# One adaLN sum moved behind a key's low part, and one weight conversion moved ahead of two copies

## The chip, the cores and the metric

The kernel runs on one NeuronCore of a Trainium2 chip. The metric is the device time of one execution in microseconds; before the change it is 1125.85 us, the median of three runs (1125.52 to 1125.99). A separate execution was taken by the hardware profiler, and all rows below come from it.

The engines of the core appear under these names: PE is TensorE (matrix products; PEld is its loading of the stationary operand), DVE is VectorE, ACT is ScalarE, POOL is GpSimd, SP is SyncE, which here only issues DMAs. Each engine works through its own instructions in order, and engines wait for each other by semaphores.

## What is computed

The reference is a two-layer trunk on one sequence of 512 tokens of 1024 channels. Cut to what matters here:

```python
def ada_modulation(c, w, b):
    m = jax.nn.silu(c) @ w + b
    shift, scale, gate = jnp.split(m, 3, axis=-1)
    ...

for i in range(DEPTH):
    shift, scale, gate = ada_modulation(c, mix_ada_w[i], mix_ada_b[i])
    h = rms_norm(x, mix_pre_g[i]) * (1.0 + scale) + shift
    y = stick_breaking_mixer(...) if i % 2 == 0 else token_mixing_mixer(...)
    x = x + gate * rms_norm(y, mix_post_g[i])
    shift, scale, gate = ada_modulation(c, ffn_ada_w[i], ffn_ada_b[i])
    h = rms_norm(x, ffn_pre_g[i]) * (1.0 + scale) + shift
    y = swiglu(h, ffn_w_gate[i], ffn_w_up[i], ffn_w_down[i])
    x = x + gate * rms_norm(y, ffn_post_g[i])
```

The mixer of layer 0 is an attention with 16 heads of 64 channels: q, k and v are products of h with `w_qkv`, the scores are turned into stick-breaking weights by a sigmoid and a running product, and the weighted sum of v goes through `w_o`. Every sublayer needs its own shift, scale and gate, each a product of the conditioning vector (1024) with a 1024 x 1024 matrix.

## The kernel before

All is float32, done on TensorE as sums of products of a high part and a low part: `split` (L109) makes the high part `h` with a copy on ScalarE and the low part `l` as source minus high part on VectorE, and `mm3` (L101) issues three products, h·h, h·l and l·h. So every weight block of 512 KB passes through ScalarE (`wh<-raw`) and VectorE (`wl<-raw`) before TensorE can use it.

**The start.** x comes in as four token tiles of 128 tokens. Each is normed, turned by TensorE into accumulator banks (`tp`, function `turn0`), and copied out by ScalarE (`turned0`) into `xhT`; one call copies the half of a tile in two instructions. Behind the copies of the first halves, ScalarE scales the turned x by the adaLN scale and shift (`high0`: `hTh<-xhT,ab`, then `xhT<-xhT,ab`); VectorE makes the low part of that (`low0`: `hTl<-xhT,hTh`). The scale and shift themselves (`ab`) are sums on VectorE (`ada_row`: `ada<-ada,scr`) over blocks that arrive by DMA (`in_ada0w`). v's first weights (`raw<-in_wv`) are split in two halves; the high part of the first half is `wh<-raw 128x512`, by an explicit instruction at L703. In this part of the program, the order on each engine is that of the code.

**The attention.** Eight pairs of heads go through a loop (`for i in range(NPAIR)`, L973). While pair i is finished, the scores of pair i + 1 are begun. For each of three groups of blocks, TensorE turns the weights of pair i (`flip`: `tw<-pack,ga`, copied out by ScalarE as `ar<-tw`), fills in other products, takes a group of scores for pair i + 1 (`z<-k,q`), which go through ScalarE's sigmoid (`ga<-z`) and VectorE's running product (the scan `ga<-ga,tri`), and fills in again. Behind the three groups stand the weighted sum of v (`values`: `av<-ar,V`) and its split (`finish`: `o<-av`).

The fillers are a generator (`filler`): first the products of q and k of the later pairs in steps of an eighth (`pqk`, read out by `evac_q` and `evac_k`), then the first part of the output product (`y<-wh,o` for two token tiles and four of the eight blocks of `w_o`). The banks for `pqk` and for the first two `y` groups come from the same two accumulator banks (tag `"p"`). `evac_k` writes k's high part on ScalarE and its low part on VectorE, both out of the bank.

The table `FILLS` (L821) says how many filler steps stand in each of the seven places of a pair (places 0 to 5 in the three groups, place 6 behind the split of o). The table `SUMS` (L824) has the same seven places and says how many steps of `bg` are taken there. `bg` computes shift, scale and gate of the first mixer's output and the next sublayer's input: three parts (G0, A0, B0) of eight blocks each, so 24 steps, each one `scalar_tensor_tensor` on VectorE that adds a block `rawada` times a column of `sc` to a running sum (`B<-rawada,sc,B`); then further steps that sum over the partitions with a product (`spare<-acch,ones`). The blocks come through two buffers (tag `raw2`), loaded by POOL's queue; the same two buffers later take the loads `rawy<-in_wy` of the feed-forward stage, issued by SP.

Four of the 24 sums are made before the loop; the loop's pairs 0 to 3 take three each, pairs 4 and 5 four each. So the last sum is the fourth of pair 5. The last filler step of q and k (the last eighth of k of pair 7) is in place 5 of pair 5.

## Time and profile before

| what | us |
|---|---|
| median of three timed runs | 1125.85 |
| the profiled execution, whole | 1127.71 |
| its span on the core | 1125.9 |
| TensorE busy | 1105.2 |
| VectorE busy | 903.2 |
| ScalarE busy | 603.0 |
| POOL busy | 39.8 |

A row of a timeline is: start and length in us, engine, line, operation, output <- inputs, shapes, count, and in brackets the idle time before it and what ended that. The names are those of the program's buffers. A line is often that of a helper (L64 for all of VectorE's and ScalarE's instructions, L90 for products, L107 for DMAs), so instructions are told apart by their buffers. "SPq" is the queue in which SP issues DMAs. A busy TensorE can still be slow: the granted clock of each stretch stands in the windows view.

### The profile page before, as it was taken

Reading aid. Unit: us, or ns where it says so; the run is one execution under the profiler, and the core shown is the slowest. Engines: PE = TensorE matmul, PEld = TensorE weight load, DVE = VectorE, ACT = ScalarE, POOL = GpSimd, SP = SyncE. Lnnn points to the kernel's source line nnn. Section 1 sums busy time; section 2 is a strip of 40 time slices with the busy share of each in tenths; the row PEclk is TensorE's granted clock in tenths of the full one; section 3 lists DMA queues with packets and bytes.
Section 4 is the critical chain, followed back from the end, with each engine's and each line's share of the span. In section 5 each row is a group of like instructions: output and inputs, shape, how many; then the busy total and the mean of one; then the engine's idle time right before and its main releaser. Section 6 shows DMA issues by size and latency. Waiting matters only on the chain.

```text
span 1125.9 us, 18286 instructions
## 1 busy us (share of the span) xinstructions
PE 1105.2 (98%) x7318; PEld 993.6 (88%) x7318; DVE 903.2 (80%) x1161; ACT 603.0 (54%) x977; POOL 39.8 (4%) x71
## 2 busy tenths in 40 slices
PE   6999999999999999999999999999999999999997
PEld 5788878779999999988878988988999999989896
DVE  7777889659988988787687774759988898889986
ACT  7646767647555555562244634437555555556552
POOL 0220111000000000010000000000000000000000
PEclk9999999999999999999999999999999999999999
DMA  9676445353244444368875482333244444223233
GB/s 361 234 216 172 145 144 168 124 187 132 76 149 150 134 132 132 110 215 270 270 255 186 159 298 83 116 113 141 84 151 127 137 132 151 75 76 112 95 94 149
DMA packets 51298, 176.09 MB, mean 156 GB/s; under 512 B 5643, under 2 KB 6155, under 8 KB 50318
## 3 DMA queue, kind: packets, MB, share of 16 engines
q1 hardware_dynamic: 45166, 153.95, 41.4%
q0 software_dynamic: 6048, 20.98, 5.9%
q8 instruction: 57, 0.93, 0.3%
q14 instruction: 27, 0.22, 0.1%
HBM read 164.43 MB, written 8.39 MB: 153 GB/s over the span
## 4 chain that ended last, share of the span: by engine, by line
PE 83%; DMA 8%; DVE 6%; issue 2%; ACT 1%; SPq 0%; POOL 0%; DVEq 0%; POOLq 0%; ACTq 0%
PE r L90 32%; PE y L90 12%; PE X L90 7%; PE v L90 7%; PE gu L90 6%; DMA rawada<-in_ada 5%; PE pqk L90 5%; PE u L90 4%; PE M L90 3%; DMA raw<-in_wdown 1%; PE z L90 1%; PE tw L98 1%; DMA ada<-in_ada0w 1%; PE av L90 1%; PE tp L98 1%
## 5 line engine op out<-in xcount | busy, mean ns | idle before, releaser
L64 ACT ACTIVATE wh<-raw 128x1024 fp32r<-128x1024 f32 (+1 forms) x112 | 116.8, 1051 | 140.9 <-PE y L90 42.0
L64 DVE TENSOR_TENSOR wl<-raw,wh 128x1024 fp32r<-128x1024 f32 (+1 forms) x112 | 134.9, 1211 | 61.9 <-ACT wh L64 61.8
L90 PE MATMUL r<-Sh,wh 128*128 128x256 f32 x608 | 170.2, 280 | 0.2 <-ACT e L64 0.2
L90 PE MATMUL r<-Sh,wl 128*128 128x256 f32 x608 | 170.4, 280 | 0.0
L90 PE MATMUL r<-Sl,wh 128*128 128x256 f32 x608 | 170.1, 280 | 0.0
L90 PE MATMUL y<-wh,as 128*128 128x512 f32 x480 | 153.3, 396 | 0.1
L64 DVE TENSOR_TENSOR wl<-f,wh 128x1024 fp32r<-128x1024 f32 x76 | 92.7, 1220 | 35.8 <-ACT wh L64 35.8
L64 ACT ACTIVATE wh<-f 128x1024 fp32r<-128x1024 f32 x76 | 80.6, 1061 | 67.9 <-PE r L90 65.1
L90 PEld LDWEIGHTS r<-Sh,wh 128*128 128x128 f32 x608 | 114.7, 189 | 0.4 <-ACT e L64 0.4
L90 PEld LDWEIGHTS r<-Sl,wh 128*128 128x128 f32 x608 | 114.6, 188 | 0.0
L90 PEld LDWEIGHTS r<-Sh,wl 128*128 128x128 f32 x608 | 114.6, 188 | 0.0
L90 PEld LDWEIGHTS y<-wh,as 128*128 128x128 f32 x480 | 90.1, 188 | 21.5 <-DVE G L64 0.6
L90 PE MATMUL y<-wl,as 128*128 128x512 f32 x240 | 94.9, 395 | 0.0
L90 PE MATMUL r<-hTh,wh 128*128 128x256 f32 x304 | 88.8, 292 | 0.2 <-DVE gu L64 0.2
L90 PE MATMUL r<-hTl,wh 128*128 128x256 f32 x304 | 84.8, 279 | 0.0
L90 PE MATMUL r<-hTh,wl 128*128 128x256 f32 x304 | 80.1, 280 | 0.0
L90 PE MATMUL X<-wh,as 128*128 128x512 f32 (+1 forms) x272 | 76.3, 356 | 0.0
L64 ACT ACTIVATE e<-r 128x256 f32<-128x256 f32 x114 | 43.4, 382 | 51.6 <-PE r L90 51.2
L90 PEld LDWEIGHTS r<-hTh,wh 128*128 128x128 f32 x304 | 57.2, 188 | 5.4 <-DVE gu L64 1.3
L90 PE MATMUL r<-hTh,b 128*128 128x256 f32 x304 | 60.7, 282 | 0.0
L64 ACT ACTIVATE wh<-rawx 128x1024 fp32r<-128x1024 f32 x38 | 40.4, 1063 | 35.9 <-PE r L90 30.8
L90 PEld LDWEIGHTS r<-hTl,wh 128*128 128x128 f32 x304 | 57.3, 188 | 0.1
(240 smaller groups left out, 2844.7 us busy)
## 6 DMA issues: line engine op xcount, KB each, us to landing
rawada<-in_ada SPq DMA_DIRECT2D x56, 512.0 KB, 5.1
raw<-in_wdown SPq DMA_DIRECT2D x44, 512.0 KB, 4.1
rawy<-in_wy SPq DMA_DIRECT2D x38, 512.0 KB, 3.6
rawx<-in_wx SPq DMA_DIRECT2D x38, 512.0 KB, 4.5
rawada<-in_ada POOLq DMA_DIRECT2D x24, 512.0 KB, 4.5
raw<-in_wqk SPq DMA_DIRECT2D x16, 512.0 KB, 4.6
ada<-in_ada0w SPq DMA_DIRECT2D x7, 1026.0 KB, 10.8
raw<-in_wgu SPq DMA_DIRECT2D x12, 512.0 KB, 3.6
```

The source lines that it names most:

```text
L64: b = f(*a, **k)
L90: b = nc.tensor.matmul(o, l, r, start=start, stop=stop, skip_group_check=True)
L98: last_tp[0] = nc.tensor.transpose(o, i, ident)
```

## The change

It has two parts. They move instructions and neither add nor remove any.

```diff
@@ -694,13 +694,14 @@
     turn0(3, 0)
     turn0(3, 1)
     ada_row(0, 1)
-    for tt in range(NT):
-        turned0(tt, 0, act)
     w, raw = wtile(2, 512), raws[0]
     wv0.append(w)
     got.append(w)
     taken[0] += 1
-    act.activation(w[0][:, 0, :], raw[:, 0, :], AF.Copy)
+    for tt in range(NT):
+        if tt == NT - 1:
+            act.activation(w[0][:, 0, :], raw[:, 0, :], AF.Copy)
+        turned0(tt, 0, act)
     high0(0)
@@ -821,7 +822,7 @@
-        SUMS = ((1, 0, 1, 0, 1, 0, 0),) * 4 + ((1, 1, 1, 0, 1, 0, 0),) * 2 + ((1, 1, 1, 1, 1, 1, 0), (1, 0, 1, 0, 1, 1, 0))
+        SUMS = ((1, 0, 1, 0, 1, 0, 0),) * 4 + ((1, 1, 1, 0, 1, 0, 0), (1, 1, 1, 0, 0, 0, 1)) + ((1, 1, 1, 1, 1, 1, 0), (1, 0, 1, 0, 1, 1, 0))
```

The first part concerns ScalarE at the start. The difference of its order (- before, + after; `xhT<-tp` are the copies of the turned x, two for each tile, the last two those of tile 3; `wh<-raw` is the high part of v's first weights; buffer numbers are serial and carry no meaning of their own):

```order
 L64 ACTIVATE xhT_117<-tp_49_195 128x2x128
 L64 ACTIVATE xhT_118<-tp_49_195 128x2x128
+L64 ACTIVATE wh_221<-raw_97 128x512
 L64 ACTIVATE xhT_117<-tp_52_209 128x2x128
 L64 ACTIVATE xhT_118<-tp_52_209 128x2x128
-L64 ACTIVATE wh_229<-raw_97 128x512
 L64 ACTIVATE hTh_121<-xhT_117,ab_205 128x512
 L64 ACTIVATE xhT_117<-xhT_117,ab_205 128x512
```

The weights' high part has moved ahead of the two copies of tile 3; what follows keeps its order. VectorE's and TensorE's order at this place is the same in both.

The second part concerns VectorE at the end of pair 5: `B<-rawada,sc,B` are the adaLN sums, `ga<-ga,tri` the scans of pair 6's scores, `k<-pqk,k` the low part of the last k, `o<-av,o` that of pair 5's output:

```order
 L64 SCALAR_TENSOR_TENSOR B_1496<-rawada_1692,sc,B_1496 128x1024
 L64 SCALAR_TENSOR_TENSOR ga_1725<-ga_1725,tri 128x256 x2
+L64 SCALAR_TENSOR_TENSOR ga_1758<-ga_1758,tri 128x512 x2
+L64 TENSOR_TENSOR k_1769<-pqk_1705,k_1769 64x512 x2
+L64 TENSOR_TENSOR o_1786<-av_717,o_1786 128x512
 L64 SCALAR_TENSOR_TENSOR B_1496<-rawada_1718,sc,B_1496 128x1024
-L64 SCALAR_TENSOR_TENSOR ga_1759<-ga_1759,tri 128x512 x2
-L64 TENSOR_TENSOR k_1770<-pqk_1705,k_1770 64x512 x2
-L64 TENSOR_TENSOR o_1787<-av_717,o_1787 128x512
 L64 TENSOR_TENSOR wl_1803<-raw_1706,wh_1802 128x1024
 L64 TENSOR_TENSOR accl_1823<-G_568,acch_1822 128x512
```

The last sum has moved behind two scans, the low part of k and the low part of o. The difference of SP's queue at the same time (`rawy` a block for the feed-forward stage, into the buffers that the `rawada` blocks leave; `g` the gains of two norms; `raw<-in_wo` output weights):

```order
 L107 DMA raw_1800<-in_wo 128x1024
 L107 DMA rawy_2511<-in_wy 128x1024
-L107 DMA rawy_2515<-in_wy 128x1024
 L107 DMA g_1820<-in_post_g 128x1024
 L107 DMA g_1892<-in_pre_g 128x1024
+L107 DMA rawy_2515<-in_wy 128x1024
 L107 DMA raw_2087<-in_wo 128x1024
 L107 DMA raw_2093<-in_wo 128x1024
```

The second `rawy` load now stands behind the two `g` loads. POOL's queue and TensorE's order are the same as before, apart from names.

## The prediction

> **What bounds the kernel now.** I read the busy times first, then what TensorE waits for, then the chain of waits around the longest of those waits, and last the granted clock there.

> ```profile
> PE 1105.2 (98%) x7318; PEld 993.6 (88%) x7318; DVE 903.2 (80%) x1161; ACT 603.0 (54%) x977; POOL 39.8 (4%) x71
> ```

> TensorE is busy for 1105.2 of 1125.9 us. The change moves no matmul, so it can win only where TensorE stands still or runs slowly. Inside the body of the kernel, the list of TensorE's waits has one long entry at the place of the second edit:

> ```profile
> PE y L90 <- DVE k L64: 2.6, 1, 2.6
> ```

> The chain of waits says where it comes from. Columns are start, length, what.

> ```profile
> 193.14 5.16 DMA rawada<-in_ada
> ...
> 203.35 0.14 issue
> 203.48 3.66 PE y L90 x9
> ...
> 231.48 20.98 PE y L90 x90
> ```

> A block of adaLN weights (`rawada`) is issued at 193.14 and lands at 193.14 + 5.16 = 198.30. Everything on the chain from there to 203.48 is VectorE, and from 203.48 it is TensorE again. The last row gives the pace of these products when nothing holds them: 20.98 / 90 = 0.233 us each. Now VectorE's timeline at this place:

> ```profile
> 195.35 1.26 DVE L64 TENSOR_TENSOR_SCAN ga<-ga,tri 128x256 f32<-128x256 f32 x2
> 198.40 1.28 DVE L64 SCALAR_TENSOR_TENSOR B<-rawada,sc,B 128x1024 f32<-128x1024 f32 x1 [1.78 <-DMA rawada<-in_ada]
> 199.60 2.33 DVE L64 TENSOR_TENSOR_SCAN ga<-ga,tri 128x512 f32<-128x512 f32 x2
> 201.94 1.39 DVE L64 TENSOR_TENSOR k<-pqk,k 64x512 fp32r<-64x512 f32 x2
> 203.37 0.69 DVE L64 TENSOR_TENSOR o<-av,o 128x512 fp32r<-128x512 f32 x1
> 203.97 1.22 DVE L64 TENSOR_TENSOR wl<-raw,wh 128x1024 fp32r<-128x1024 f32 x1
> ...
> 208.38 2.34 DVE L64 TENSOR_TENSOR_SCAN ga<-ga,tri 128x512 f32<-128x512 f32 x2 [1.45 <-ACT ga L64]
> ```

> The last adaLN sum (198.40) stands ahead of the scans and of the low part of the last k (201.94). VectorE idles 1.78 us for its weights and spends 1.28 us on it. Only when the second half of k has been read out of the accumulator bank can TensorE start the second group of `y`, which takes that same bank.

> **The change, part by part: the adaLN sum.** The sum goes behind the scans, k and the split of o. Then the scans no longer wait for the DMA. They need ScalarE's sigmoids, and k needs ScalarE's high part:

> ```profile
> 195.20 1.09 ACT L64 ACTIVATE ga<-z 128x512 f32<-128x512 f32 x2 [0.52 <-PE z L90]
> 197.07 1.21 ACT L64 ACTIVATE k<-pqk 64x512 fp32r<-64x512 f32 x2 [0.78 <-PE pqk L90]
> 199.40 0.60 ACT L64 ACTIVATE o<-av 128x512 fp32r<-128x512 f32 x1 [1.12 <-PE av L90]
> 200.82 1.06 ACT L64 ACTIVATE wh<-raw 128x1024 fp32r<-128x1024 f32 x1
> ```

> The sigmoids are done at 196.29 and VectorE at 195.35 + 1.26 = 196.61, where a successor starts some 0.08 before the listed end (199.60 against 198.40 + 1.28), so the scans start at 196.53. k follows 201.94 - 199.60 = 2.34 later, at 198.87, after its high part (197.07 + 1.21 = 198.28), and takes 1.39: 200.26. With the 0.14 of the chain, the bank is free for TensorE at **200.40**. TensorE's own rows:

> ```profile
> 200.46 0.39 PE L90 MATMUL y<-wh,o 128*128 128x512 f32 x1
> ...
> 203.48 0.77 PE L90 MATMUL y<-wh,o 128*128 128x512 f32 x1 [2.63 <-DVE k L64]
> ...
> 206.98 0.22 PE L90 MATMUL z<-k,q 128*128 128x128 f32 x1
> ...
> 210.40 0.40 PE L90 MATMUL y<-wl,o 128*128 128x512 f32 x1
> ```

> The last product ahead of the wait starts at 200.46, the next could start at 200.46 + 0.233 = 200.69, and the bank is free 0.29 before that. **First term: 203.48 - 200.69 = 2.79 us.** The wait vanishes as a whole, with 0.29 to spare.

> Second term: after the wait TensorE is slow. Nine products go from 203.48 to 206.98, 3.50 us, where 9 x 0.233 = 2.10 would do. The windows show why (columns: window, length, busy times, then granted clock, DMA share, GB/s):

> ```profile
> 200.90:203.40 2.50, 0.00 (x0) 0.00 (x0) 2.44 (x4) 2.44 (x4) 0.00 (x0) 0.92 0.82 292
> 203.40:204.00 0.60, 0.52 (x1) 0.50 (x2) 0.60 (x2) 0.00 (x0) 0.00 (x0) 0.50 0.96 246
> ...
> 206.00:206.50 0.50, 0.50 (x2) 0.38 (x2) 0.50 (x1) 0.00 (x0) 0.00 (x0) 0.60 0.79 156
> 206.50:207.00 0.50, 0.50 (x4) 0.39 (x3) 0.43 (x1) 0.00 (x0) 0.00 (x0) 1.00 0.86 188
> ```

> The clock is halved: 0.92 over 2.50 us means the last 0.4 us of the wait, and 0.60 over 0.50 us means up to about 206.4. Half of the 2.9 us between 203.48 and 206.4 is about 1.45, which agrees. **Second term: 3.50 - 2.10 = 1.40 us**, gone if the wait that sets the clock back is gone. Sum: 2.79 + 1.40 = **4.19 us**.

> What is late next? Behind the moved sum on VectorE's queue stand the low part of the fourth output weight (203.97), the low part of G, another weight and the next scans (208.38). o is split from 200.26 to 200.95 (its high part is there at 200.00), the sum runs from 200.87 to 202.15 with its weights long landed, and the low part, which waits for ScalarE's high part (200.82 + 1.06 = 201.88), goes from 202.07 to 203.29. TensorE asks for it at 210.40, or at 206.21 once it is 4.19 earlier: 2.9 us of cover. Then 0.61 and 1.22 us for the two next (0.69 and 1.22 listed) put the scans at 204.97. 208.38 - 4.19 = 204.19 would be their moved time; they come 0.78 late, and their reader on TensorE is the transposing of the next pair, more than 8 us away, so I take nothing for it. On SyncE's queue the second `rawy` load waits for the sum, so it moves from about 199.7 to 202.2, and the two `g` loads pass it; the weight load behind it waits for the low part (205.2 before, 203.3 now). The queue's row, and the first reader of `rawy`:

> ```profile
> 195.46 4.58 SPq L107 DMA_DIRECT2D rawy<-in_wy  x2
> ```

> ```profile
> L64 ACT ACTIVATE b<-rawy x2: 619/620/621, 274.5 to 275.1; 128x512 fp32r<-128x512 f32 x2
> ```

> All these cost nothing while they keep their covers. From 207 on the chain of waits is TensorE up to 252, so 4.19 us travels on.

> **The high part of v's first weights.** It goes ahead of the copies of the last token tile. In order: SyncE's issue, the DMA's time to landing, ScalarE and VectorE.

> ```profile
> 4.24 0.44 SPq L107 DMA_DIRECT2D raw<-in_wv  x1
> ```

> ```profile
> raw<-in_wv SPq DMA_DIRECT2D x1, 512.0 KB, 9.8
> ```

> ```profile
> 14.08 0.66 ACT L64 ACTIVATE xhT<-tp 128x256 f32<-128x256 f32 x2 [0.79 <-PE tp L98]
> 14.62 0.63 ACT L64 ACTIVATE wh<-raw 128x512 fp32r<-128x512 f32 x1
> 15.14 0.81 ACT L64 ACTIVATE hTh<-xhT,ab 128x512 fp32r<-128x512 f32 x1
> 15.99 0.82 ACT L64 ACTIVATE xhT<-xhT,ab 128x512 f32<-128x512 f32 x1
> 16.77 1.23 DVE L64 SCALAR_TENSOR_TENSOR ada<-ada,scr 128x1026 f32<-128x1026 f32 x1 [0.79 <-DMA ada<-in_ada0w]
> 17.92 0.69 DVE L64 TENSOR_TENSOR hTl<-xhT,hTh 128x512 fp32r<-128x512 f32 x1
> ```

> ScalarE idles 0.79 us ahead of 14.08, and the edit means to fill that. But the weights land at 4.24 + 9.8 = 14.04, so ScalarE would wait there instead: high part near 14.08, copies at 14.60, scaled x at 14.60 + 0.66 = about 15.28 instead of 15.14. If they were there at 13.3, scaled x would come near 14.78, 0.36 earlier. Neither matters for the end as I read it: VectorE's queue waits for another load until 16.77 and reaches the low part of x at 17.92, for which ScalarE's 15.99 + 0.82 = 16.81 is 1.1 us early. TensorE's next products need that low part. **Term: 0.** Bounds: VectorE's idle of 0.79 is all that an earlier landing could win (-0.79), and the two copies, now behind the weights, are all that a later one could expose (+0.66). I keep both for the range.

> The profiled execution took 1127.71 us with its span of 1125.9, so it would go to 1127.71 - 4.19 = 1123.52. The three timed runs have a median of 1125.85, 1.86 below it; I take the same difference off that: **1121.66 us**, which is 0.37% less.

> **The rivals.** First, the gap closes, but the timed runs never paid for the clock. A wait of the same length elsewhere left it at full speed (last figure but two of a window):

> ```profile
> 569.92 0.50 PE L90 MATMUL adaps<-acch,ones 128*128 128x512 f32 x1 [2.66 <-ACT acch L64]
> ```

> ```profile
> 569.00:570.00 1.00, 0.08 (x1) 0.08 (x1) 0.62 (x1) 1.00 (x3) 0.00 (x0) 1.00 0.88 356
> ```

> So 2.6 us may or may not halve the clock, and the 1.86 us that the profiled execution is slower could hold these 1.40. Then only 2.79 is won: 1123.06. [...]

> Second, the gain is swallowed later. TensorE's 2.66 us wait at 569.92 ends a stretch in which the chain goes from DMA to DMA. Had that stretch a clock of its own, TensorE would wait there 4.19 longer, and the time stays at 1125.85. But its head hangs on TensorE, so it should start earlier by as much:

> ```profile
> 470.63 12.99 PE r L90 x107
> 483.64 0.13 ACT gu L64
> ```

> Third, slower: the sum keeps waiting for its DMA and now holds up another queue of work.

> ```profile
> DMA to landing us min/median/max: 3.7/4.5/9.9
> ```

> VectorE waits if the weights land after 200.87 (7.7 us after issue), and TensorE if the low part of the fourth weight ends after 206.2, which is a landing after about 203.6, 10.5 us after issue. Each further us costs one; the whole 4.19 is gone at 207.8, 14.7 after issue, and a landing at 211 gives 1125.85 + 3.2 = 1129. For it: the `g` loads may now leave from 195.8 on, while `rawada` is in flight. Against it: 1 MB more at the 292 GB/s of the first window above is 3.6 us, a landing at 201.9 at worst, and the longest of 24 took 9.9.

> **How the numbers follow.** Forecast as summed, 1121.66: 0.50. Clock not paid for, 1123.06: 0.30. Swallowed later, or a new short wait that leaves under 2.25 us of gain: 0.16. Slower: 0.04. A measurement of this kernel can tell about 0.2%, 2.25 us; both of the first cases exceed it. So faster 0.80, same 0.16, slower 0.04. The range runs from 1121.66 - 0.79 = 1120.9 to 1123.06 + 0.66 = 1123.7, opened to 1120.7 and 1123.8 because the three runs themselves lie between 1125.52 and 1125.99.

> **What would show it.** Right: TensorE's list of waits has no `y` behind `k`; k's low part starts near 198.9 with no idle ahead of the scans; the moved sum starts near 200.9; the granted clock stays at 1.00 through 200 to 207, and z starts near 202.8 instead of 206.98. For the first edit: ScalarE's high part starts at about 14.1 behind a DMA wait, with hTl still at 17.9. Wrong: a new wait of TensorE between 203 and 232, a `y` that waits for `wl`, or a wait at 570 that has grown to some 6.9 us.

## The result, and the profile after

The changed kernel takes 1123.2 us, the median of 20 runs (1120.92 to 1124.78); the kernel before takes 1125.4 us in 20 runs (1122.23 to 1127.48). The ratio is 0.9977, with a 95% interval of 0.9970 to 0.9985: 2.6 us won (1.7 to 3.4), where 4.19 were forecast as likeliest and 2.79 as the next case. The two medians by themselves lie 2.2 us apart; the ratio is taken from all the runs. The profiled executions lie further apart, 1122.0 against 1125.9 us of span.

TensorE's list of waits of the changed kernel, in total, times and longest, whole:

```profile
PE sc L90 <- ACT sc L64: 2.9, 1, 2.9
PE v L90 <- ACT hTh L64: 2.5, 3, 1.4
PE tp L98 <- DVE x L64: 2.2, 2, 1.5
PE adaps L90 <- ACT acch L64: 2.0, 1, 2.0
PE v L90 <- DVE hTl L64: 1.3, 2, 0.8
PE r L90 <- ACT e L64: 0.3, 1, 0.3
```

The `y` that waited for `k` is gone from it. VectorE's timeline at the place of the sum:

```profile
195.26 3.50 DVE L64 TENSOR_TENSOR_SCAN ga<-ga,tri 128x256 f32<-128x256 f32 x4
198.77 1.39 DVE L64 TENSOR_TENSOR k<-pqk,k 64x512 fp32r<-64x512 f32 x2
200.19 0.69 DVE L64 TENSOR_TENSOR o<-av,o 128x512 fp32r<-128x512 f32 x1
200.80 1.28 DVE L64 SCALAR_TENSOR_TENSOR B<-rawada,sc,B 128x1024 f32<-128x1024 f32 x1
201.99 1.22 DVE L64 TENSOR_TENSOR wl<-raw,wh 128x1024 fp32r<-128x1024 f32 x1
203.13 0.69 DVE L64 TENSOR_TENSOR accl<-G,acch 128x512 fp32r<-128x512 f32 x1
203.73 1.22 DVE L64 TENSOR_TENSOR wl<-raw,wh 128x1024 fp32r<-128x1024 f32 x1
204.87 2.33 DVE L64 TENSOR_TENSOR_SCAN ga<-ga,tri 128x512 f32<-128x512 f32 x2
```

No row has idle time before it. All four scans run as one piece, k's low part starts at 198.77, and the sum, at 200.80, finds its weights landed. The low part of the fourth output weight ends at 203.21, and the next scans start at 204.87. TensorE there, from the chain of waits (start, length, what), and the next score:

```profile
199.26 0.80 PE tw L98 x6
200.06 2.79 PE y L90 x12
202.86 1.14 PE z L90 x8
```

```profile
202.69 0.22 PE L90 MATMUL z<-k,q 128*128 128x128 f32 x1
```

Twelve products of `y` follow each other at 2.79 / 12 = 0.233 us, so z starts at 202.69 instead of 206.98. The windows (granted clock last but two) have no fall of the clock:

```profile
203.00:204.00 1.00, 1.00 (x8) 1.00 (x7) 1.00 (x3) 0.80 (x2) 0.00 (x0) 1.00 0.91 274
204.00:205.00 1.00, 1.00 (x6) 0.78 (x6) 1.00 (x2) 0.64 (x2) 0.00 (x0) 1.00 1.02 307
```

But later in the same execution, behind the wait near 565 (2.01 us) that stood near 570 before (2.66 us) and left the clock alone there, the clock is halved:

```profile
565.00:566.00 1.00, 0.98 (x3) 0.81 (x4) 1.00 (x2) 1.00 (x2) 0.00 (x0) 0.77 0.93 381
566.00:567.00 1.00, 1.00 (x4) 0.74 (x3) 1.00 (x2) 0.46 (x2) 0.00 (x0) 0.50 0.62 184
567.00:568.00 1.00, 1.00 (x4) 0.81 (x3) 0.65 (x1) 0.18 (x1) 0.00 (x0) 0.50 0.72 217
```

So two single executions cannot give the size of the gain; the experiments take that up. The start of the changed kernel, ScalarE and VectorE:

```profile
13.69 0.63 ACT L64 ACTIVATE wh<-raw 128x512 fp32r<-128x512 f32 x1 [0.23 <-DMA raw<-in_wv]
14.22 0.64 ACT L64 ACTIVATE xhT<-tp 128x256 f32<-128x256 f32 x2
14.75 0.81 ACT L64 ACTIVATE hTh<-xhT,ab 128x512 fp32r<-128x512 f32 x1
14.35 0.69 DVE L64 TENSOR_TENSOR wl<-raw,wh 128x512 fp32r<-128x512 f32 x1
16.70 1.23 DVE L64 SCALAR_TENSOR_TENSOR ada<-ada,scr 128x1026 f32<-128x1026 f32 x1 [1.66 <-DMA ada<-in_ada0w]
17.86 0.69 DVE L64 TENSOR_TENSOR hTl<-xhT,hTh 128x512 fp32r<-128x512 f32 x1
```

ScalarE now waits for the weights, as foreseen, and scaled x comes 0.39 us earlier than before. The edit also reaches VectorE by another way: the low part of the same weights (`wl<-raw,wh`) needs that high part, and before the change VectorE waited for it:

```profile
15.29 0.69 DVE L64 TENSOR_TENSOR wl<-raw,wh 128x512 fp32r<-128x512 f32 x1 [0.75 <-ACT wh L64]
```

Now it starts 0.94 us earlier, without a wait. VectorE turns that into a longer idle time ahead of the load that it hangs on (0.75 + 0.79 = 1.54 us of idle in two places before, 1.66 in one place now), and hTl starts at 17.86 against 17.92.

### The profile page after: what moved, and what is told of

The parts are those of the page before. It is cut to its first block, busy times and chain, and to the rows that moved or that the text cites. A ratio compares the mean times of both kernels' runs of the same rounds, so it can differ in the third digit from the quotient of the medians.

```text
span 1122.0 us, 18286 instructions
## 1 busy us (share of the span) xinstructions
PE 1104.4 (98%) x7318; PEld 993.9 (89%) x7318; DVE 903.3 (81%) x1161; ACT 603.4 (54%) x977; POOL 39.8 (4%) x71
## 3 DMA queue, kind: packets, MB, share of 16 engines
q0 software_dynamic: 6048, 20.98, 6.0%
## 4 chain that ended last, share of the span: by engine, by line
PE 88%; DMA 6%; DVE 3%; ACT 2%; issue 1%; SPq 0%; DVEq 0%; ACTq 0%
PE r L90 33%; PE y L90 12%; PE X L90 7%; PE v L90 7%; PE pqk L90 7%; PE gu L90 6%; PE u L90 4%; DMA rawada<-in_ada 3%; PE M L90 3%; PE z L90 2%; PE av L90 2%; PE tw L98 2%; DMA raw<-in_wdown 1%; DMA ada<-in_ada0w 1%; PE tp L98 1%; PE sv L90 1%
## 5 line engine op out<-in xcount | busy, mean ns | idle before, releaser
L64 ACT ACTIVATE wh<-raw 128x1024 fp32r<-128x1024 f32 (+1 forms) x112 | 117.0, 1051 | 138.3 <-PE y L90 45.6
L64 DVE TENSOR_TENSOR wl<-raw,wh 128x1024 fp32r<-128x1024 f32 (+1 forms) x112 | 135.0, 1211 | 59.4 <-ACT wh L64 57.9
L90 PE MATMUL r<-Sh,wh 128*128 128x256 f32 x608 | 170.2, 280 | 0.3 <-ACT e L64 0.3
L90 PE MATMUL r<-Sh,wl 128*128 128x256 f32 x608 | 170.4, 280 | 0.0
L90 PE MATMUL r<-Sl,wh 128*128 128x256 f32 x608 | 170.1, 280 | 0.0
L90 PE MATMUL y<-wh,as 128*128 128x512 f32 x480 | 154.0, 398 | 0.0
L64 DVE TENSOR_TENSOR wl<-f,wh 128x1024 fp32r<-128x1024 f32 x76 | 92.8, 1220 | 35.8 <-ACT wh L64 35.8
L64 ACT ACTIVATE wh<-f 128x1024 fp32r<-128x1024 f32 x76 | 80.7, 1061 | 67.9 <-PE r L90 64.8
L90 PEld LDWEIGHTS r<-Sh,wh 128*128 128x128 f32 x608 | 114.7, 189 | 0.5 <-ACT e L64 0.5
L90 PEld LDWEIGHTS r<-Sl,wh 128*128 128x128 f32 x608 | 114.6, 189 | 0.0
L90 PEld LDWEIGHTS r<-Sh,wl 128*128 128x128 f32 x608 | 114.6, 189 | 0.0
L90 PEld LDWEIGHTS y<-wh,as 128*128 128x128 f32 x480 | 90.7, 189 | 21.3
L90 PE MATMUL y<-wl,as 128*128 128x512 f32 x240 | 95.5, 398 | 0.0
L90 PE MATMUL r<-hTh,wh 128*128 128x256 f32 x304 | 88.8, 293 | 0.0
L90 PE MATMUL r<-hTl,wh 128*128 128x256 f32 x304 | 84.8, 279 | 0.0
L90 PE MATMUL r<-hTh,wl 128*128 128x256 f32 x304 | 80.1, 280 | 0.0
L90 PE MATMUL X<-wh,as 128*128 128x512 f32 (+1 forms) x272 | 76.2, 356 | 0.0
L64 ACT ACTIVATE e<-r 128x256 f32<-128x256 f32 x114 | 43.4, 382 | 51.9 <-PE r L90 51.7
L90 PEld LDWEIGHTS r<-hTh,wh 128*128 128x128 f32 x304 | 57.2, 188 | 5.1 <-DVE gu L64 0.9
L90 PE MATMUL r<-hTh,b 128*128 128x256 f32 x304 | 60.7, 282 | 0.0
L64 ACT ACTIVATE wh<-rawx 128x1024 fp32r<-128x1024 f32 x38 | 40.4, 1062 | 36.5 <-PE r L90 30.8
L90 PEld LDWEIGHTS r<-hTl,wh 128*128 128x128 f32 x304 | 57.3, 188 | 0.1
## 6 DMA issues: line engine op xcount, KB each, us to landing
rawada<-in_ada SPq DMA_DIRECT2D x56, 512.0 KB, 4.7
raw<-in_wdown SPq DMA_DIRECT2D x44, 512.0 KB, 4.0
rawy<-in_wy SPq DMA_DIRECT2D x38, 512.0 KB, 3.6
rawx<-in_wx SPq DMA_DIRECT2D x38, 512.0 KB, 4.3
rawada<-in_ada POOLq DMA_DIRECT2D x24, 512.0 KB, 4.5
raw<-in_wqk SPq DMA_DIRECT2D x16, 512.0 KB, 4.2
raw<-in_wgu SPq DMA_DIRECT2D x12, 512.0 KB, 3.5
```

The lines of the kernel that those rows point to most:

```text
L64: b = f(*a, **k)
L90: b = nc.tensor.matmul(o, l, r, start=start, stop=stop, skip_group_check=True)
```

## The experiments

**The two parts alone.** One kernel takes the table entry only, one the start only.

```diff
# the sum only
-    ... + ((1, 1, 1, 0, 1, 0, 0),) * 2 + ...
+    ... + ((1, 1, 1, 0, 1, 0, 0), (1, 1, 1, 0, 0, 0, 1)) + ...
# the start only
     for tt in range(NT):
+        if tt == NT - 1:
+            act.activation(w[0][:, 0, :], raw[:, 0, :], AF.Copy)
         turned0(tt, 0, act)
```

> Only the table entry is changed (the adaLN sum behind the last k), the start is that of before. My theory: the start edit is worth nothing, so this takes what the whole change takes, a ratio to before of about 0.9977 (-2.8 us where the clock was not halved before, -4.2 where it was); TensorE has no wait for k, z starts near 202.7. Rival, the start edit costs or wins up to 0.7 us: then this lies 0.0006 beside the whole change.

> Only the high part of v's first weights is moved. My theory: 0 (ratio 1.0000 within the interval); hTl still starts near 17.9 and TensorE waits 2.6 us for k near 201. Whether the clock then falls to a half is open: if it falls, z is 3.5 us behind the first product after the wait, else 2.1. Rival: scaled x some 0.4 us earlier carries through, -0.4 us (0.9996).

The sum alone has a ratio of 0.9975 (0.9964 to 0.9986), as the whole change. The start alone has 1.0009 (0.9996 to 1.0021). Its profile keeps the wait, and yet not the slow products:

```profile
203.07 0.48 PE L90 MATMUL y<-wh,o 128*128 128x512 f32 x1 [2.69 <-DVE k L64]
...
205.25 0.22 PE L90 MATMUL z<-k,q 128*128 128x128 f32 x1
```

From the first product behind the wait to z are 2.18 us, not 3.50. The clock did not fall (1.00 in every microsecond from 200 to 208), with a wait no shorter than the one profiled before (2.69 against 2.63). All of the gain comes from the sum; the start edit gives nothing that can be measured. The timed interval alone would still admit the rival's 0.4 us, at its edge. The profiles say more: in the ten executions of the table further down, the first score of the attention starts at 58.22 us on average in the four with the start edit and at 58.29 in the six without.

**The wait filled.** Extra products into a bank that is not in use yet, so that TensorE is busy while it waits for k.

```diff
+    if tt == 3 and k == 0 and hf == 1:
+        for _ in range(11):
+            mm(spare[:], o8[0][:, 0, tok], w[0][:, 0, c], True, True)
     mm3(y[hf][:], ...)
```

> Before, with eleven extra products into a bank whose contents are not used (the spare bank, before its first use) set into TensorE's wait for k: 11 x 0.233 = 2.56 us of a wait of 2.63. The wait for k stays, but TensorE is not idle. My theory: the clock stays at 1.00, the nine products after k take 2.10 instead of 3.50 us, z starts near 205.6; timed, 1.40 us times the share of executions in which the clock of before falls: 0.9988 if in all, 1.0000 if in none, about 0.9993 if in half. Rival, that the slow products have another cause than the idle time (the DMA traffic of that moment): still 3.5 us, ratio 1.0000.

```profile
201.09 2.72 PE L90 MATMUL spare<-wh,o 128*128 128x512 f32 x11
203.86 0.47 PE L90 MATMUL y<-wh,o 128*128 128x512 f32 x1
...
206.02 0.22 PE L90 MATMUL z<-k,q 128*128 128x128 f32 x1
```

The nine products take 206.02 - 203.86 = 2.16 us, at a clock of 1.00. One execution shows little by this, since the clock also stayed up in the start-only one, where nothing filled the wait. Timed, the ratio is 0.9996 (0.9987 to 1.0005): 0.45 us won, between 1.5 won and 0.6 lost. This measures the clock term by itself, in timed runs: it does not exclude zero, and the whole 1.40 lies at its edge.

**The DMA wait without the order.** The last block of weights gets a buffer of its own and is loaded long ahead; the order is that of before.

```diff
-    raw = fwork["raw"].tile([P, D], F32, tag="raw2", name=nm("rawada"))[:]
+    if len(self.todo) == 1 and self.queue is nc.gpsimd:
+        raw = fwork["own"][:]
+    else:
+        raw = fwork["raw"].tile([P, D], F32, tag="raw2", name=nm("rawada"))[:]
```

> Before, with a buffer of its own for the last block of adaLN weights, so that it is loaded long ahead (the small pool has 3 instead of 4 buffers to make room). The order stays that of before: the sum in front of scans and k. This takes away the DMA wait of 1.78 us and leaves the sum's 1.20. My theory: the sum starts near 196.5, k is out near 201.5, TensorE's wait for k shrinks from 2.6 to about 0.9, too short for the clock to fall; 1.75 us won and the share of 1.40 that the clock costs: ratio about 0.998. Rival, that the order and not the DMA makes the wait: the wait stays above 2 us.

```profile
197.02 1.26 DVE L64 SCALAR_TENSOR_TENSOR B<-rawadaown,sc,B 128x1024 f32<-128x1024 f32 x1
198.19 2.33 DVE L64 TENSOR_TENSOR_SCAN ga<-ga,tri 128x512 f32<-128x512 f32 x2
200.54 1.39 DVE L64 TENSOR_TENSOR k<-pqk,k 64x512 fp32r<-64x512 f32 x2
```

```profile
202.08 0.48 PE L90 MATMUL y<-wh,o 128*128 128x512 f32 x1 [0.74 <-DVE k L64]
```

The sum no longer waits, and TensorE's wait shrinks to 0.74 us: the DMA made most of it, the sum's own time the rest. The ratio is 0.9981 (0.9972 to 0.9990), 2.1 us (1.1 to 3.2), so, as far as two such intervals can tell, most of the change's gain comes without the change of order.

**The start with its cover taken away.** The load that VectorE hangs on at 16.7 is cut in two halves, with the whole change and with the sum only.

```diff
-    if k:
+    if k > 1:
         load(raw[:], A["ada0w"][k])
     else:
         for i in range(2):
             load(raw[:, i, :], A["ada0w"][k, :, i])
```

> The whole change, and the second block of the first adaLN weights (ada, 1 MB) loaded as two halves of 512 KB, of which VectorE's first sum needs one. My theory of the start: VectorE's queue hangs on this load (16.70) and not on ScalarE, so the sum starts near 15.3 and the chain to 29.7 moves by up to 1.3 us: 1 us less than the whole change, ratio to before about 0.9968. Rival: the loads behind it (the next weights of v, which ScalarE waits for until 21.8) set the end of the start, and the ratio stays at 0.9977.

> As the run with the halved load, but with the start's order on ScalarE of before: the high part of v's first weights behind the last copies. The load that hid the start edit is early here, so its cover is gone. My theory: hTl now waits for ScalarE and starts near 16.8 instead of 16.1 (0.5 to 0.7 us later than with the start edit); timed about 0.0005 above that run, 0.9967. Rival, the start edit is worth nothing here either: hTl at 16.1, 0.9962.

VectorE in the first and in the second of these:

```profile
14.13 0.68 DVE L64 TENSOR_TENSOR wl<-raw,wh 128x512 fp32r<-128x512 f32 x1
14.73 1.22 DVE L64 SCALAR_TENSOR_TENSOR ada<-ada,scr 128x1026 f32<-128x1026 f32 x1
...
16.10 0.69 DVE L64 TENSOR_TENSOR hTl<-xhT,hTh 128x512 fp32r<-128x512 f32 x1
...
20.44 1.23 DVE L64 SCALAR_TENSOR_TENSOR ada<-ada,scr 128x1026 f32<-128x1026 f32 x1 [0.55 <-DMA ada<-in_ada0w]
```

```profile
15.15 0.69 DVE L64 TENSOR_TENSOR wl<-raw,wh 128x512 fp32r<-128x512 f32 x1 [0.75 <-ACT wh L64]
15.76 1.22 DVE L64 SCALAR_TENSOR_TENSOR ada<-ada,scr 128x1026 f32<-128x1026 f32 x1
...
16.91 0.69 DVE L64 TENSOR_TENSOR hTl<-xhT,hTh 128x512 fp32r<-128x512 f32 x1
...
20.51 1.22 DVE L64 SCALAR_TENSOR_TENSOR ada<-ada,scr 128x1026 f32<-128x1026 f32 x1
```

With the start edit hTl comes 0.81 us earlier. About 0.2 of that is not the edit's: the norm of the last token tile, ahead of all this, already starts 0.19 earlier in that execution (12.19 against 12.38). The remaining 0.6 lies in the forecast 0.5 to 0.7, but by another way than forecast: without the edit it is `wl` that waits 0.75 us for ScalarE, and hTl follows the sum without a wait of its own. Four microseconds later the lead is lost: VectorE waits for the next block, and the sums stand at 20.44 and 20.51. The first score of the attention starts at 57.42 and 57.48 (58.16 to 58.41 in the three executions of the change alone). Timed: 0.9962 (0.9950 to 0.9975) with the start edit, 0.9965 (0.9952 to 0.9979) without. So the halved load was worth 0.7 to 1.0 us at the first score in the profiles, and its kernel, with a median of 1121.2 us in 5 runs, has the lowest median of all here; but its interval overlaps that of the change, so the timed runs do not show this gain. The start edit is worth nothing there either.

**The same kernels again.** Six more executions were profiled, four of before and two of the whole change.

> Before once more, for the clock alone. My theory: whether the clock is halved after the wait for k is chance from one execution to the next, as the wait (2.6 us) stays the same; if it falls, the nine products after the wait take 3.5 us, else 2.1. Rival, the clock falls in every execution at this place: 3.5 us.

> Before once more, for the clock alone, with the same expectations as the other look at before.

> Before, one execution more, to see what the wait near 201 and the stretch from z (near 206) to the first v product of the second layer (near 652) take. So far: wait 2.05 to 2.81 us, clock fallen in 3 of 4, stretch 444.0 to 446.6 us. My theory: the clock falls by chance, in some two of three executions, and the stretch is the same for before and after (it holds another wait, near 570, that varies by itself). Rival: the stretch is longer after the change, by the 1 to 1.5 us that the timed gain falls short of 4.2.

> Before, one execution more, with the same expectations as the other look at before: wait 2.0 to 2.8 us, clock fallen or not, stretch 444 to 447 us.

> The whole change, one execution more. No wait for k, clock 1.00 between 200 and 208, z between 202.3 and 202.8. My theory: the stretch from z to the first v product of the second layer takes 444 to 447 us, as before the change. Rival: 446.5 to 447.5 in every execution, 1 us or more above those of before.

> The whole change, one execution more, with the same expectations as the other look at it: no wait for k, stretch 444 to 447 us, or 446.5 to 447.5 by the rival.

One of them, called before (4) in the table: TensorE, then the windows.

```profile
202.91 0.47 PE L90 MATMUL y<-wh,o 128*128 128x512 f32 x1 [2.12 <-DVE k L64]
...
205.76 0.31 PE L90 MATMUL z<-k,q 128*128 128x128 f32 x1
```

```profile
203.00:204.00 1.00, 1.00 (x5) 0.82 (x6) 1.00 (x2) 0.28 (x1) 0.00 (x0) 1.00 0.66 262
204.00:205.00 1.00, 1.00 (x5) 0.76 (x4) 1.00 (x2) 0.00 (x0) 0.00 (x0) 0.62 0.94 385
205.00:206.00 1.00, 1.00 (x5) 0.80 (x4) 1.00 (x2) 0.00 (x0) 0.00 (x0) 0.50 0.70 197
206.00:207.00 1.00, 1.00 (x6) 1.00 (x5) 0.36 (x1) 0.00 (x0) 0.00 (x0) 0.50 0.83 242
207.00:208.00 1.00, 1.00 (x6) 0.98 (x5) 0.30 (x1) 0.61 (x2) 0.00 (x0) 0.67 0.78 254
```

The wait is shorter (2.12 us), and the clock falls more than a microsecond after TensorE has begun to work again: 0.62 over the second row means a fall at 204.24, and 0.67 over the last a return at 207.66, 3.4 us later. The executions of before, of the whole change and of its two parts, read from such rows (all but the clock in us):

| execution | VectorE idle for the weights | TensorE's wait for k | clock fell there | first score to z | z to first v product |
|---|---|---|---|---|---|
| before | 1.78 | 2.63 | yes | 148.48 | 446.43 |
| start only | 1.84 | 2.69 | no | 147.23 | 446.60 |
| before (2) | 1.96 | 2.81 | yes | 148.86 | 444.01 |
| before (3) | 1.21 | 2.05 | yes, late | 147.40 | 446.33 |
| before (4) | 1.27 | 2.12 | yes, late | 147.32 | 447.31 |
| before (5) | 1.30 | 2.15 | no | 146.69 | 445.67 |
| whole change | 0 | 0 | no | 144.28 | 447.06 |
| sum only | 0 | 0 | no | 144.29 | 446.43 |
| whole change (2) | 0 | 0 | no | 144.28 | 444.63 |
| whole change (3) | 0 | 0 | no | 144.28 | 445.50 |

The first score is that at 58.50 in the profile before, z the one at 206.98, and the first v product the start of the second layer's v products in the chain of waits, 653.41. With the sum moved, the stretch up to z is 144.28 us each time, within 0.01. With the wait it varies by 2.2 us, and its mean is 147.66. The stretch behind z has a mean of 446.06 with the wait and 445.91 without: the gain is not given back there in these executions. The single values range over 3 us, so this rules out that the whole gain is given back, but not a loss of 1 us.

## Why the prediction was right, and what was mis-sized

**The mechanism** of the sum's move was right at each step: k, o and the sum stand where the sum of times put them (198.77, 200.19, 200.80 against 198.87, 200.26, 200.87), TensorE's wait is gone, the DMA wait and the sum's time both stood behind it (the own buffer separates them), and what queues behind the sum comes in time. The rival of a late landing did not occur: in each of the six profiles with the sum moved, VectorE does not wait for the weights. The rival that the gain is swallowed near 570 finds nothing for it in the table's last column; TensorE's wait there is 2.01, 0.43 and 1.62 us with the whole change, not some 6.9.

**The first term**, 2.79 us, was read from one execution and treated as fixed. Its DMA part is not: in six executions VectorE waited 1.21 to 1.96 us for the same weights and TensorE 2.05 to 2.81 for k. Where the clock did not fall, the stretch up to z was 2.41 and 2.95 us longer than 144.28.

**The second term**, 1.40 us, is the step that was mis-sized: the forecast took it as paid in every execution, with half the chance on that, though the row at 569.92 had shown a like wait without it. In the six executions with the wait the clock fell in four, in two of them so late that part of it fell on the work behind z; the filled wait puts its timed worth at 0.45 us with an interval of 1.5 to -0.6. TensorE worked at half clock behind the wait for 2.92, 3.34, 3.41 and 3.41 us in those four; half of that, spread over all six executions, is an estimate of 1.1 us, inside that interval. By the profiles, wait and clock together cost 147.66 - 144.28 = 3.38 us on average up to z. The timed 2.6 (1.7 to 3.4) and the median of 1123.2 are close to the forecast's second case, the clock not paid for (2.79 and 1123.06). That case did not come true as it was meant, though: the clock was paid for in four of six profiled executions, so the agreement of the numbers is in part luck. Why the timed gain is 0.8 below that of six and four profiles is not settled; single executions of one kernel differ by more than 5 us here, so the profiles' mean is itself loose.

**The start edit** was right at nothing, for the reason given: the load at 16.7 sets the time. In the change's profile its weights landed at 4.26 + 9.4 = 13.66, not 14.04, so scaled x came 0.39 us earlier rather than 0.14 later; neither reached the end. Two things the prediction did not see. The edit works through the low part of the weights on VectorE, whose wait of 0.75 us for ScalarE the prediction's rows leave out. And a second load stands behind the first: with the first out of the way, what the edit won ended in the wait at 20.44.

## What to carry to other kernels

When TensorE waits for an engine that itself waits for a DMA in the middle of its queue, move the instruction that needs the DMA behind those that TensorE needs, or load earlier: here the one took the wait of 2.63 us away, the other left 0.74 of it. Count a fall of the clock behind a wait as a chance, not as a price (here it fell in four of six executions, with waits of 2.05 to 2.81 us), and profile a second execution before adding it to a sum. Filling one engine's idle time was worth nothing that can be measured here (1.0009, 0.9996 to 1.0021) while another engine's queue waited for a later load (VectorE, until 16.7); in the profiles, halving that load brought the attention forward by 0.7 to 1.0 us and the edit did not.

## What was not expected of the hardware

The clock fell to half after waits of 2.05 and 2.12 us, stayed full after waits of 2.15 and 2.69 in executions of the same products (and of 2.66 near 570), and fell at different distances from the wait: about 0.5 us before its end in the first profile, over 1 us after it in before (4). In the own buffer's execution it fell behind a wait of 1.80 us near 566, to 0.50 from 568 to 570:

```profile
566.46 0.50 PE L90 MATMUL adaps<-acch,ones 128*128 128x512 f32 x1 [1.80 <-ACT acch L64]
```

| execution | TensorE's wait, from and to | most of it in one stretch | clock fell |
|---|---|---|---|
| before (2) | 200.50 to 203.31 | 2.74 | yes |
| before | 200.85 to 203.48 | 2.14 | yes |
| before (4) | 200.79 to 202.91 | 2.08 | yes |
| before (3) | 200.71 to 202.76 | 2.05 | yes |
| whole change | 563.01 to 565.02 | 2.01 | yes |
| own buffer | 564.66 to 566.46 | 1.80 | yes |
| before | 567.26 to 569.92 | 1.70 | no |

In the profiles before and of the whole change, from 20 us on, the clock falls at the end of every stretch with 2.01 us or more of idle time and of none with 1.70 or less, and no stretch lies between. With the own buffer it fell after one with 1.80. In the first 20 us it fell at 9.16 with the whole change (2.19 us idle in that stretch), at 9.28 with the halved load (at most 1.87) and at 9.36 in before (3) (at most 1.95). Start only, sum only, whole change (3), before (5) and the halved load with the sum only had waits of 1.59 to 2.69 us without a fall; how much of these lies in one stretch is not shown. The DMA traffic, the rival named at the filled wait, does not sort the cases: with the whole change its share was 0.91 and 1.02 between 203 and 205, without a fall. So, as far as the rows of the table go, a fall goes with where the wait lies against the stretches. As an estimate, with the 1.80 us taken as the border and the 3.41 us as fixed, a wait of 2.1 us, placed at random, would bring a fall in a little over half of the executions, one of 2.8 us in about three quarters; four of six were seen. No run here moved the stretches on purpose; this is read from the traces alone.
